# A hybrid decoder block on one core: more stages between the hops of a transposed block, the last gate block transposed on TensorE, and one bias and one mask product per head

## The chip, the cores and the metric

The kernel runs on one core of one Trainium2 chip. The metric is device time in microseconds (us), from launch to end; the median of three runs is 1239.57 us. PE is the matmul engine (TensorE), PEld its weight load, DVE the vector engine, ACT the scalar engine, POOL GpSimd, and SP the engine whose queue issues most of the loads.

## The reference, cut to what matters

One decoder block on a sequence of 256 positions with 2048 channels, all in float32:

```
h    = rms_norm(x) @ w_in                      # attention q, k, v; forget gate; mLSTM q, k, v, i, f, o
attn = softmax(q k^T / sqrt(128) + c_q - c_k, causal) @ v        # 8 heads of 128, c = cumsum(log f)
ht   = mlstm_chunkwise(silu(conv(mq, mk)), mv, i, log f)         # 4 heads, q/k 128, v 256
x   += concat(attn, rms_norm(ht) * sigmoid(mo)) @ w_out
x   += (silu(h2 @ w_gate) * (h2 @ w_up)) @ w_down                # h2 = rms_norm(x), 5632 columns
x   += sigmoid(rms_norm(x) @ w_ple_gate) * rms_norm(p @ w_ple_proj)
```

## The kernel before

Every large product goes through `linear`. The 256 positions are two query blocks of 128, each with a PSUM accumulator of 128 x 512. A weight piece of 256 rows by 512 columns is loaded by SP into `wr` (512 KB), ACT casts it to `wh` (fp32r), and DVE takes the rest, `wl = wr - wh`. Each 128 rows then give three matmuls per query block (L253 to L255: activation high by wh, high by wl, low by wh), so one piece is 12 matmuls. The pool of `wr`, `wh` and `wl` has four buffers of each.

The activations must stand with channels on the partitions, as pairs `act_h` and `act_l` of 512 channels (four of 128) by 256 positions. Two ways lead there:

- `transposed` goes by hops. DVE transposes 32 x 32 squares into `tq` (two instructions), ACT's queue issues four stores to a DRAM tile `swap` (L191) and one load from it into `quad` (L195), and `split` takes high and low parts from `quad` (ACT L133 or L129, DVE L135 or L130). `tq` and `quad` have one buffer each, and the list `held` lets only one block be under way.
- `transpose_in` transposes on TensorE, four 128 x 128 products with the identity (L165) into a PSUM tile `tr`, then `split`; it does two channel groups at a time. The first activations and the second half of the mLSTM output go this way.

Such side work is written as tasks, generators that `advance` steps: before each weight piece `linear` calls `advance(width)`, which takes one step of up to `width` tasks (2 in most linears, 1 in the feed-forward part and w_down). Each `yield` is the end of a step. Before a linear uses an activation block whose task is not done, it steps the tasks until it is. The order of instructions on each engine is fixed when the program is built, from the dependences and the program's order as a priority, so an instruction can be placed ahead of earlier ones; at run time each engine keeps its order.

Stages in order: the projections of w_in (with attention, convolution and mLSTM as tasks beside them), w_out, eleven chunks of gate and up, w_down, four short linears of w_ple_proj (one piece each, results `e` copied by ACT at L678, squared by the task `e_norm`), and w_ple_gate with the output. `residual` runs w_out ("ffn") and w_down ("ple") in four chunks of 512 columns: the DVE addition into `xres` (L616), then the task `after`, whose hops give the activation block for the next product. The block of w_down's chunk 3 is needed by w_ple_gate's seventh piece.

For the heads, `bias_mms` adds to the scores of query block b the bias product of a one-row selector `sel` with the table `R` (128 or 256 columns, L473) and the product of a bf16 identity with the bf16 mask `maskb` (128 columns, L474). `attn` runs the q-k products before it (L541, two instructions each in the trace), `mlstm` keeps bias and q-k products in two tiles (q-k at L495).

Of the kernel before, what the change touches and what calls it, by code (L numbers as in the profile page):

```python
# [14 lines left out]
P = 128  # L15
EPS = 1e-6
NEG = -1e30


def block_kernel(ctx, tc, x, p, w_norm_mix, w_in, fox_f_bias, q_norm_w, k_norm_w, conv_w, conv_b,  # L20
# [147 lines left out]
    def transpose_in(dst, srcs, k0, n, scales=None):  # L168

        for j0 in range(0, n, 2):  # L170
            if j0:
                yield
            t = transpose_pair(lambda b, j: srcs(b, j0 + j))
            split(dst, k0 + j0, 2, t, scales and scales[j0:j0 + 2])

    held = []

    def transposed(srcs):

        while held:
            yield held
        held.append(srcs)
        t = quads.tile([P, 2, 4, 4, 32], F32, name="tq")
        for b in range(2):
            nc.vector.transpose(t[:, b], srcs(b).rearrange("p (k j c) -> p j k c", k=4, j=4))
        yield
        d = dram.tile([4, 32, 2, 4, P], F32, name="swap")
        for i in range(4):  # L190
            nc.scalar.dma_start(out=d[:, :, :, i, :].rearrange("j c b e -> c b j e"),  # L191
                                in_=t[32 * i:32 * i + 32].rearrange("c b j k r -> c b j (k r)"))
        yield
        q = quads.tile([P, 8, 4, 32], F32, name="quad")
        nc.scalar.dma_start(out=q.rearrange("p t k r -> p (t k r)"), in_=d.rearrange("j c b i e -> (j c) (b i e)"))  # L195
        yield
        return q.rearrange("p t k r -> p k t r")

    def split_by_blocks(dst, srcs, scales=None):

        tv = yield from transposed(srcs)
        for k in range(0, 4, 2):
            split(dst, k, 2, tv[:, k:k + 2], scales and scales[k:k + 2])
            if not k:
                yield
        held.pop()
# [52 lines left out]
    with tc.tile_pool(name="mixp", bufs=1) as mp:  # L259
# [125 lines left out]
        for c in range(3):  # L385
            po = linear(w_in, acts_x, 4104 + c * 344, 344)
            for b in range(2):
# [7 lines left out]
        Ch = mp.tile([P, P], F32, name="Ch")  # L395
        sel = mp.tile([P, 12], F32R, name="sel")
        identb = mp.tile([P, P], BF16, name="identb")
        maskb = mp.tile([P, P], BF16, name="maskb")
        nc.gpsimd.memset(ones, 1.0)
        nc.gpsimd.affine_select(out=Ut, in_=ones, compare_op=ALU.is_ge, fill=0.0, base=0, pattern=[[1, P]],  # L400
                                channel_multiplier=-1)
# [2 lines left out]
                                channel_multiplier=-1)  # L404
        nc.gpsimd.tensor_tensor(out=Uc, in0=Ut, in1=Ch, op=ALU.add)
        nc.gpsimd.tensor_tensor(out=Un, in0=Ut, in1=ones, op=ALU.subtract)
        nc.gpsimd.memset(maskb, 0.0)
        nc.gpsimd.affine_select(out=maskb, in_=maskb, compare_op=ALU.is_ge, fill=NEG, base=0, pattern=[[-1, P]],
                                channel_multiplier=1)
        make_identity(nc, identb)  # L410
        sel0 = mp.tile([P, 12], F32, name="sel0")
        nc.gpsimd.memset(sel0, 0.0)
# [54 lines left out]

        NK = (P, 2 * P)

        def bias_mms(t, b, h, start):  # L470

            r0 = 0 if b == 0 else 128
            nc.tensor.matmul(t[:, b, 0:NK[b]], sel[:, h:h + 1].broadcast_to([P, P]), R[:, r0:r0 + NK[b]], start=start, stop=False)  # L473
            nc.tensor.matmul(t[:, b, b * P:(b + 1) * P], identb, maskb, start=False, stop=True)  # L474

        def transpose_probs(src):

# [9 lines left out]
        rh = mp.tile([P, 2, 4], F32, name="rh")  # L487

        def mlstm(h):
            pD = ps.tile([P, 2, 256], F32, name="sc")  # L490
            for b in range(2):
                bias_mms(pD, b, 8 + h, True)
            pS = ps.tile([P, 2, 256], F32, name="sc")
            for b in range(2):
                nc.tensor.matmul(pS[:, b, 0:NK[b]], cv[:, h, b * P:(b + 1) * P], cv[:, 4 + h, 0:NK[b]], start=True, stop=True)  # L495
            mx = small.tile([P, 2], F32, name="mx")
            eb = small.tile([P, 2], F32, name="eb")
            em = small.tile([P, 2], F32, name="em")
            den = small.tile([P, 2], F32, name="den")
            for b in range(2):  # L500
                nc.vector.tensor_reduce(mx[:, b:b + 1], pD[:, b, 0:NK[b]], axis=AX.X, op=ALU.max)
            nc.vector.tensor_tensor(mx, mx, ncT[:, :, h], op=ALU.subtract)
            nc.vector.scalar_tensor_tensor(mx, nBT[:, :, h], -1.0, mx, op0=ALU.mult, op1=ALU.max)
            nc.vector.scalar_tensor_tensor(eb, ncT[:, :, h], -1.0, mx, op0=ALU.mult, op1=ALU.subtract)
            nc.scalar.activation(em, mx, AF.Exp, scale=-1.0)
            W = mp.tile([P, 2, 256], F32, name="prob", bufs=2)
            for b in range(2):
                nc.scalar.activation(W[:, b, 0:NK[b]], pD[:, b, 0:NK[b]], AF.Exp, bias=eb[:, b:b + 1])
                nc.vector.scalar_tensor_tensor(W[:, b, 0:NK[b]], pS[:, b, 0:NK[b]], 1.0, W[:, b, 0:NK[b]],
                                               op0=ALU.mult, op1=ALU.mult, accum_out=den[:, b:b + 1])  # L510
            nc.vector.scalar_tensor_tensor(den, den, -1.0, den, op0=ALU.mult, op1=ALU.max)
            nc.vector.tensor_tensor(den, den, em, op=ALU.max)
            nc.vector.reciprocal(den, den)
            yield
            WT = transpose_probs(W)
            yield
            ph = ps.tile([P, 2, 256], F32, name="tr")
            vs = slice(h * 256, (h + 1) * 256)
            nc.tensor.matmul(ph[:, 0, :], WT[:, 0:128], sB[:, 0, vs], start=True, stop=True)
            nc.tensor.matmul(ph[:, 1, :], WT[:, 128:256], sB[:, 0, vs], start=True, stop=False)  # L520
            nc.tensor.matmul(ph[:, 1, :], WT[:, 256:384], sB[:, 1, vs], start=False, stop=True)
            for b in range(2):
                nc.scalar.activation(hm[:, b, vs], ph[:, b, :], AF.Copy, scale=den[:, b:b + 1])
                sumsq(ssh[:, b, h:h + 1], hm[:, b, vs])
# [11 lines left out]
        acts_m = [None] * 4  # L536

        def attn(h, qT, kT, v):
            t = ps.tile([P, 2, 256], F32, name="sc")
            for b in range(2):  # L540
                nc.tensor.matmul(t[:, b, 0:NK[b]], qT[:, h % 4, b * P:(b + 1) * P], kT[:, h % 4, 0:NK[b]], start=True,  # L541
                                 stop=False)
                bias_mms(t, b, h, False)
            nm = small.tile([P, 2], F32, name="nm")
            rsum = small.tile([P, 2], F32, name="rsum")
            pb = mp.tile([P, 2, 256], F32, name="prob", bufs=2)
            for b in range(2):
                nc.vector.tensor_reduce(nm[:, b:b + 1], t[:, b, 0:NK[b]], axis=AX.X, op=ALU.max, negate=True)
                nc.scalar.activation(pb[:, b, 0:NK[b]], t[:, b, 0:NK[b]], AF.Exp, bias=nm[:, b:b + 1],
                                     accum_out=rsum[:, b:b + 1])  # L550
            nc.vector.reciprocal(rsum, rsum)
            for b in range(2):
                nc.vector.tensor_scalar(pb[:, b, 0:NK[b]], pb[:, b, 0:NK[b]], rsum[:, b:b + 1], None, ALU.mult)
            yield
            pT = transpose_probs(pb)
            yield
            o = ps.tile([P, 1, 256], F32, name="tr")
            vs = slice((h % 4) * P, (h % 4 + 1) * P)
            nc.tensor.matmul(o[:, 0, :], v[:, 0, vs], pT[:, 0:256], start=True, stop=False)  # L559
            nc.tensor.matmul(o[:, 0, 128:256], v[:, 1, vs], pT[:, 256:384], start=False, stop=True)  # L560
            split(acts_m[h // 4], h % 4, 1, o)
# [34 lines left out]
        def residual(w, acts, voff, name, pieces=None):  # L596

            ss = const.tile([P, 2, 4], F32, name="ss_" + name)
            rstd = const.tile([P, 2], F32, name="rstd_" + name)

            def after(c, dst):
                scales = [vec_b[:, voff + c * 4 + j:voff + c * 4 + j + 1] for j in range(4)]
                yield from split_by_blocks(dst, lambda b: xres[:, b, c * 512:(c + 1) * 512], scales)
                for b in range(2):
                    sumsq(ss[:, b, c:c + 1], xres[:, b, c * 512:(c + 1) * 512])
                if c == 3:
                    ssr = small.tile([P, 2], F32, name="ssr")
                    nc.vector.tensor_reduce(ssr, ss, axis=AX.X, op=ALU.add)
                    rsqrt(rstd, ssr, 1.0 / D, [P, 2])

            nxt = []
            for c in range(4):
                cs = slice(c * 512, (c + 1) * 512)
                po = linear(w, acts, c * 512, 512, pieces=pieces, width=1 if pieces else 2)
                for b in range(2):
                    nc.vector.tensor_tensor(xres[:, b, cs], po[b], xres[:, b, cs], op=ALU.add)  # L616
                nxt.append(new_act())
                made_by[id(nxt[c][0])] = Task(after(c, nxt[c]))
            return nxt, rstd
# [104 lines left out]
```

## Time and profile before

| | us |
|---|---|
| median of three runs (lowest, highest) | 1239.57 (1239.51, 1240.84) |
| the profiled execution's own time | 1238.18 |
| its span, first to last instruction | 1236.5 |
| PE busy | 1219.0 |
| DVE busy | 708.2 |
| ACT busy | 587.7 |

The span is what the profiler saw between the first and the last instruction; the device time has 1.7 us around it. Busy time is the union of an engine's instructions. Matmuls overlap in the records and their ends are modelled, so a busy PE is not a PE at its best rate: the distance from one start to the next tells more. In the rows below, the bracket at the end of a timeline row is the idle time of the engine just before it and what ended it; x2 or x4 means that neighbouring instructions of one line were merged.

### The profile page before, as it was taken

To read this page: it belongs to the slowest core of one execution; us is meant where nothing else is said; L and a number is where in the kernel's file an instruction comes from. 1 tells how busy PE (TensorE), PEld (TensorE's weight loads), DVE (VectorE), ACT (ScalarE), POOL (GpSimd) and SP (SyncE) were. 2 spreads that over 40 slices of the span, in tenths; PEclk is the share of its full clock that TensorE was granted. 3 is DMA by queue.
4 is the path that set the end of the run, shared out by engine and by line. 5 is a ranking of instruction groups with operands and counts; after the bars stand their busy time and mean duration, and the time that the engine had idled before them with its cause. 6 is when DMAs were issued, how large, how long until landed. Compare 5 with 4: busy or idle time off the path is not lost.

```text
span 1236.5 us, 15306 instructions
## 1 busy us (share of the span) xinstructions
PE 1219.0 (99%) x5691; PEld 1020.2 (83%) x5691; DVE 708.2 (57%) x950; ACT 587.7 (48%) x822; POOL 4.1 (0%) x23
## 2 busy tenths in 40 slices
PE   9999999999999999999999999999999999998998
PEld 6799977888888888888888888888888888887788
DVE  5567655565665755555555555556545554544764
ACT  6655555555545534444443443444344444445542
POOL 1000000000000000000000000000000000000000
PEclk9999999999999999999999999999999999999999
DMA  7577754665678776777777777677766666765772
GB/s 259 175 239 230 223 158 120 187 214 165 216 230 255 226 223 201 232 209 215 227 222 213 213 223 219 201 227 221 221 211 211 210 212 203 224 198 172 221 242 90
DMA packets 160013, 258.35 MB, mean 209 GB/s; under 512 B 10082, under 2 KB 56004, under 8 KB 159940
## 3 DMA queue, kind: packets, MB, share of 16 engines
q1 hardware_dynamic: 127156, 229.06, 60.4%
q10 hardware_dynamic: 32784, 28.33, 7.5%
q8 instruction: 44, 0.72, 0.2%
q14 instruction: 29, 0.24, 0.1%
HBM read 241.62 MB, written 15.73 MB: 208 GB/s over the span
## 4 chain that ended last, share of the span: by engine, by line
PE 80%; ACT 2%; DMA 2%; DVE 1%; issue 0%; ACTq 0%; DVEq 0%
PE acc L254 26%; PE acc L255 26%; PE acc L253 26%; DMA swap<-tq 1%; DMA quad<-swap 1%; ACT sq L116 1%; DVE wl L229 0%; ACT wh L228 0%; PE sc L541 0%; DMA wr<-in_w_in_dram 0%; PE tr L559 0%; ACT qs L344 0%; ACTq L191 0%; PE tr L479 0%; PE sc L495 0%
## 5 line engine op out<-in xcount | busy, mean ns | idle before, releaser
L229 DVE TENSOR_TENSOR wl<-wr,wh 128x1024 fp32r<-128x1024 f32 (+2 forms) x445 | 521.3, 1181 | 409.4 <-ACT wh L228 408.6
L228 ACT CAST wh<-wr 128x1024 fp32r<-128x1024 f32 (+2 forms) x445 | 448.0, 1018 | 518.8 <-PE acc L255 370.9
L253 PE MATMUL acc<-wh,act_h 128*128 128x512 f32 (+2 forms) x1568 | 592.9, 379 | 5.7 <-ACT wh L228 4.6
L254 PE MATMUL acc<-wl,act_h 128*128 128x512 f32 (+2 forms) x1568 | 592.2, 378 | 4.7 <-DVE wl L229 4.7
L255 PE MATMUL acc<-wh,act_l 128*128 128x512 f32 (+2 forms) x1568 | 591.9, 377 | 0.0
L254 PEld LDWEIGHTS acc<-wl,act_h 128*128 128x128 f32 x1568 | 295.3, 188 | 57.5 <-DVE wl L229 6.9
L253 PEld LDWEIGHTS acc<-wh,act_h 128*128 128x128 f32 x1568 | 294.7, 188 | 57.9 <-ACT wh L228 5.7
L255 PEld LDWEIGHTS acc<-wh,act_l 128*128 128x128 f32 x1568 | 295.0, 188 | 51.8 <-DVE act_l L135 0.6
L253 PE MATMUL acc<-wh,gh 128*128 128x512 f32 x224 | 88.0, 393 | 0.0
L254 PE MATMUL acc<-wl,gh 128*128 128x512 f32 x224 | 87.9, 393 | 0.0
L255 PE MATMUL acc<-wh,gl 128*128 128x512 f32 x224 | 87.1, 389 | 0.0
L255 PEld LDWEIGHTS acc<-wh,gl 128*128 128x128 f32 x224 | 42.0, 188 | 9.5
L253 PEld LDWEIGHTS acc<-wh,gh 128*128 128x128 f32 x224 | 42.1, 188 | 9.4
L254 PEld LDWEIGHTS acc<-wl,gh 128*128 128x128 f32 x224 | 42.1, 188 | 8.6
L133 ACT ACTIVATE act_h<-quad,vec_b 128x256 fp32r<-128x256 f32 x36 | 15.5, 499 | 23.1 <-DMA quad<-swap 23.1
L135 DVE SCALAR_TENSOR_TENSOR act_l<-quad,vec_b,act_h 128x256 fp32r<-128x256 f32 x36 | 15.3, 483 | 17.6 <-ACT act_h L133 17.6
L637 ACT ACTIVATE gg<-acc,rstd_ffn 128x512 f32<-128x512 f32 x22 | 15.1, 689 | 10.8 <-PE acc L255 10.8
L638 DVE SCALAR_TENSOR_TENSOR gg<-acc,rstd_ffn,gg 128x512 f32<-128x512 f32 x22 | 15.8, 751 | 4.9 <-ACT gg L637 4.9
L130 DVE TENSOR_TENSOR gl<-quad,gh 128x512 fp32r<-128x512 f32 x14 | 9.1, 688 | 16.3 <-ACT gh L129 16.3
L129 ACT CAST gh<-quad 128x512 fp32r<-128x512 f32 x14 | 8.0, 618 | 20.5 <-DMA quad<-swap 20.5
L641 DVE SCALAR_TENSOR_TENSOR gg<-acc,rstd_ffn,gg 128x512 f32<-128x512 f32 x22 | 15.4, 744 | 0.0
L116 ACT ACTIVATE sq<-xres 128x512 bf16<-128x512 f32 x24 | 14.9, 622 | 0.0
(192 smaller groups left out, 398.1 us busy)
## 6 DMA issues: line engine op xcount, KB each, us to landing
wr<-in_w_ffn_gate_dram SPq DMA_DIRECT2D x88, 512.0 KB, 3.8
wr<-in_w_ffn_up_dram SPq DMA_DIRECT2D x88, 512.0 KB, 4.6
wr<-in_w_ffn_down_dram SPq DMA_DIRECT2D x88, 512.0 KB, 4.6
wr<-in_w_in_dram SPq DMA_DIRECT2D x63, 512.0 KB, 4.5
wr<-in_w_in_dram SPq DMA_DIRECT2D x48, 344.0 KB, 3.7
wr<-in_w_out_dram SPq DMA_DIRECT2D x32, 512.0 KB, 4.7
wr<-in_w_ple_gate_dram SPq DMA_DIRECT2D x32, 512.0 KB, 5.0
swap<-tq ACTq DMA_DIRECT2D x104, 128.0 KB, 4.2
```

The source lines that it names most:

```text
L116: nc.scalar.activation(sq[:, 0:n], src, AF.Square, accum_out=dst)
L130: nc.vector.tensor_tensor(lo, src, hi.bitcast(F32), op=ALU.subtract)
L133: nc.scalar.activation(part(dst[0], k + j, 1), src[:, j:j + 1], AF.Copy, scale=scales[j])
L135: nc.vector.scalar_tensor_tensor(part(dst[1], k + j, 1), src[:, j:j + 1], scales[j], part(dst[0], k + j, 1).bitcast(F32), op0=ALU.mult, op ...
L228: nc.scalar.copy(wh, wr)
L229: nc.vector.tensor_tensor(wl, wr, wh.bitcast(F32), op=ALU.subtract)
L253: nc.tensor.matmul(po[b][:, 0:n], ah[:, kk, s], wh[:, j, :], start=count == 1, stop=False)
L254: nc.tensor.matmul(po[b][:, 0:n], ah[:, kk, s], wl[:, j, :], start=False, stop=False)
L255: nc.tensor.matmul(po[b][:, 0:n], al[:, kk, s], wh[:, j, :], start=False, stop=count == total)
L637: nc.scalar.activation(gg[b], pg[b], AF.Sigmoid, scale=r)
L638: nc.vector.scalar_tensor_tensor(gg[b], pg[b], r, gg[b], op0=ALU.mult, op1=ALU.mult)
L641: nc.vector.scalar_tensor_tensor(gg[b], pu[b], rstd2[:, b:b + 1], gg[b], op0=ALU.mult, op1=ALU.mult)
```

## The change

Three edits go together.

- `transposed` takes a parameter `gap` (2 unless given). After the swap issues and after the quad issue it now ends `gap` steps in place of one. `split_by_blocks` hands it on; chunk 3 of w_out keeps gap 1.
- Chunk 3 of w_down, the last block, goes through `transpose_in`: eight TensorE transposes from `xres`, with no hop through DRAM.
- Scores stand in one tile of 512 columns: block 0 in columns 0 to 127, block 1 in 128 to 383 (`keys`). One bias product of 384 columns and one mask product of 256 (columns 0 to 127 and 256 to 383, from a mask of two copies, made by one more instruction on POOL) serve both query blocks. In `attn` the bias comes first, then the q-k products, then the mask.

```diff
-    def transposed(srcs):
+    def transposed(srcs, gap=2):
...
             nc.scalar.dma_start(out=d[:, :, :, i, :].rearrange("j c b e -> c b j e"),
                                 in_=t[32 * i:32 * i + 32].rearrange("c b j k r -> c b j (k r)"))
-        yield
+        for _ in range(gap):
+            yield
         q = quads.tile([P, 8, 4, 32], F32, name="quad")
         nc.scalar.dma_start(out=q.rearrange("p t k r -> p (t k r)"), in_=d.rearrange("j c b i e -> (j c) (b i e)"))
-        yield
+        for _ in range(gap):
+            yield
         return q.rearrange("p t k r -> p k t r")
...
-        tv = yield from transposed(srcs)
+        tv = yield from transposed(srcs, gap)
...
-        def bias_mms(t, b, h, start):
-
-            r0 = 0 if b == 0 else 128
-            nc.tensor.matmul(t[:, b, 0:NK[b]], sel[:, h:h + 1].broadcast_to([P, P]), R[:, r0:r0 + NK[b]], start=start, stop=False)
-            nc.tensor.matmul(t[:, b, b * P:(b + 1) * P], identb, maskb, start=False, stop=True)
+        def keys(t, b):
+
+            return t[:, 0:P] if b == 0 else t[:, P:3 * P]
+
+        def bias_mm(t, h):
+
+            nc.tensor.matmul(t[:, 0:3 * P], sel[:, h:h + 1].broadcast_to([P, P]), R, start=True, stop=False)
+
+        def mask_mm(t):
+
+            nc.tensor.matmul(t.rearrange("p (a c) -> p a c", c=P)[:, 0:3:2, :], identb, maskb2, start=False, stop=True)
...
-            pD = ps.tile([P, 2, 256], F32, name="sc")
-            for b in range(2):
-                bias_mms(pD, b, 8 + h, True)
+            pD = ps.tile([P, 512], F32, name="sc")
+            bias_mm(pD, 8 + h)
+            mask_mm(pD)
...
-            t = ps.tile([P, 2, 256], F32, name="sc")
-            for b in range(2):
-                nc.tensor.matmul(t[:, b, 0:NK[b]], qT[:, h % 4, b * P:(b + 1) * P], kT[:, h % 4, 0:NK[b]], start=True,
-                                 stop=False)
-                bias_mms(t, b, h, False)
+            t = ps.tile([P, 512], F32, name="sc")
+            bias_mm(t, h)
+            for b in range(2):
+                nc.tensor.matmul(keys(t, b), qT[:, h % 4, b * P:(b + 1) * P], kT[:, h % 4, 0:NK[b]], start=False, stop=False)
+            mask_mm(t)
...
-                yield from split_by_blocks(dst, lambda b: xres[:, b, c * 512:(c + 1) * 512], scales)
+                if c == 3 and name == "ple":
+                    yield from transpose_in(dst, lambda b, j: xres[:, b, c * 512 + j * P:c * 512 + (j + 1) * P], 0, 4, scales)
+                else:
+                    yield from split_by_blocks(dst, lambda b: xres[:, b, c * 512:(c + 1) * 512], scales, 1 if c == 3 else 2)
```

## Rows read from the trace of the kernel before

**Rows 1.** The page, busy time by engine (us, share, instructions).

```profile
PE 1219.0 (99%) x5691; PEld 1020.2 (83%) x5691; DVE 708.2 (57%) x950; ACT 587.7 (48%) x822; POOL 4.1 (0%) x23
```

**Rows 2.** PE's timeline, last gate block (start, us, instruction, idle before).

```profile
1136.84 0.39 PE L255 MATMUL acc<-wh,pl 128*128 128x512 f32 x1
1138.18 0.73 PE L253 MATMUL acc<-wh,act_h 128*128 128x512 f32 x2 [0.95 <-ACT wh L228]
...
1139.77 0.39 PE L255 MATMUL acc<-wh,act_l 128*128 128x512 f32 x1
...
1141.61 0.39 PE L255 MATMUL acc<-wh,act_l 128*128 128x512 f32 x1
1143.70 0.73 PE L253 MATMUL acc<-wh,act_h 128*128 128x512 f32 x2 [1.70 <-ACT wh L228]
...
1145.56 0.63 PE L255 MATMUL acc<-wh,act_l 128*128 128x512 f32 x1
...
1148.12 0.46 PE L253 MATMUL acc<-wh,act_h 128*128 128x512 f32 x1
```

**Rows 3.** PE's waits: who for whom, us in total, times, longest.

```profile
PE acc L254 <- DVE wl L229: 4.7, 6, 2.0
PE acc L253 <- ACT wh L228: 4.6, 3, 1.9
```

**Rows 4.** The waits of all engines, ACT's for the stores to swap.

```profile
ACT wh L228 <- DMA swap<-tq: 44.2, 19, 3.0
```

**Rows 5.** Window of 20 us (busy us by engine, granted clock, DMA share, GB/s).

```profile
1140.00:1160.00 20.00, 17.77 (x70) 13.93 (x69) 13.78 (x26) 13.18 (x25) 0.00 (x0) 0.91 0.68 203
```

**Rows 6.** ACT's timeline, last gate block (ACTq is its sequencer).

```profile
1129.03 1.93 ACTq L191 DMA_DIRECT2D swap<-tq  x3
...
1135.48 0.33 ACTq L195 DMA_DIRECT2D quad<-swap  x1
1135.86 0.63 ACT L116 ACTIVATE sq<-act_h 128x512 bf16<-128x512 f32 x1 [0.75 <-DMA swap<-tq]
...
1137.10 1.03 ACT L228 CAST wh<-wr 128x1024 fp32r<-128x1024 f32 x1
1138.82 0.91 ACT L133 ACTIVATE act_h<-quad,vec_b 128x256 fp32r<-128x256 f32 x2 [0.70 <-DMA quad<-swap]
...
1142.61 1.04 ACT L228 CAST wh<-wr 128x1024 fp32r<-128x1024 f32 x1
```

**Rows 7.** Chain of waits, the mLSTM output's second block on TensorE.

```profile
320.88 0.44 PE tr L165 x4
```

**Rows 8.** PE's timeline, one mLSTM head and one attention head.

```profile
169.43 0.22 PE L473 MATMUL sc<-R,sel 128*128 128x128 f32 x1
...
169.80 0.87 PE L495 MATMUL sc<-m 128*128 128x128 f32 x4
170.33 0.58 PE L253 MATMUL acc<-wh,act_h 128*128 128x512 f32 x1
...
281.04 0.30 PE L473 MATMUL sc<-R,sel 128*128 128x128 f32 x1
...
282.13 0.30 PE L473 MATMUL sc<-R,sel 128*128 128x128 f32 x1
```

**Rows 9.** PE's timeline, 256-column matmuls of the last linear.

```profile
1224.83 0.28 PE L255 MATMUL acc<-wh,act_l 128*128 128x256 f32 x1
...
1227.95 0.28 PE L254 MATMUL acc<-wl,act_h 128*128 128x256 f32 x1
```

**Rows 10.** PE's timeline, its two long stalls beside the projections.

```profile
59.48 0.59 PE L253 MATMUL acc<-wh,act_h 128*128 128x344 f32 x2 [1.90 <-ACT wh L228]
...
114.92 0.43 PE L254 MATMUL acc<-wl,act_h 128*128 128x344 f32 x1 [2.00 <-DVE wl L229]
```

**Rows 11.** DVE's timeline after the convolution steps.

```profile
113.99 3.23 DVE L229 TENSOR_TENSOR wl<-wr,wh 128x688 fp32r<-128x688 f32 x4
```

**Rows 12.** PE's timeline, first scores of the second half.

```profile
269.60 0.49 PE L541 MATMUL sc<-qkT 128*128 128x128 f32 x2 [0.33 <-ACT qkT L326]
```

More of the change, by code (lines that the diff above doesn't have):

```diff
@@ L192, in transposed, with split_by_blocks @@
                                 in_=t[32 * i:32 * i + 32].rearrange("c b j k r -> c b j (k r)"))
-        yield
+        for _ in range(gap):
+            yield
         q = quads.tile([P, 8, 4, 32], F32, name="quad")
         nc.scalar.dma_start(out=q.rearrange("p t k r -> p (t k r)"), in_=d.rearrange("j c b i e -> (j c) (b i e)"))
-        yield
+        for _ in range(gap):
+            yield
         return q.rearrange("p t k r -> p k t r")
-    def split_by_blocks(dst, srcs, scales=None):
-        tv = yield from transposed(srcs)
+    def split_by_blocks(dst, srcs, scales=None, gap=2):
+        tv = yield from transposed(srcs, gap)
         for k in range(0, 4, 2):
@@ L397, in block_kernel @@
         identb = mp.tile([P, P], BF16, name="identb")
-        maskb = mp.tile([P, P], BF16, name="maskb")
+        maskb2 = mp.tile([P, 2, P], BF16, name="maskb")
         nc.gpsimd.memset(ones, 1.0)
@@ L406, in block_kernel @@
         nc.gpsimd.tensor_tensor(out=Un, in0=Ut, in1=ones, op=ALU.subtract)
-        nc.gpsimd.memset(maskb, 0.0)
-        nc.gpsimd.affine_select(out=maskb, in_=maskb, compare_op=ALU.is_ge, fill=NEG, base=0, pattern=[[-1, P]],
-                                channel_multiplier=1)
+        nc.gpsimd.memset(maskb2, 0.0)
+        for b in range(2):
+            nc.gpsimd.affine_select(out=maskb2[:, b, :], in_=maskb2[:, b, :], compare_op=ALU.is_ge, fill=NEG, base=0,
+                                    pattern=[[-1, P]], channel_multiplier=1)
         make_identity(nc, identb)
@@ L489, in mlstm @@
         def mlstm(h):
-            pD = ps.tile([P, 2, 256], F32, name="sc")
+            pD = ps.tile([P, 512], F32, name="sc")
+            bias_mm(pD, 8 + h)
+            mask_mm(pD)
+            pS = ps.tile([P, 512], F32, name="sc")
             for b in range(2):
-                bias_mms(pD, b, 8 + h, True)
-            pS = ps.tile([P, 2, 256], F32, name="sc")
-            for b in range(2):
-                nc.tensor.matmul(pS[:, b, 0:NK[b]], cv[:, h, b * P:(b + 1) * P], cv[:, 4 + h, 0:NK[b]], start=True, stop=True)
+                nc.tensor.matmul(keys(pS, b), cv[:, h, b * P:(b + 1) * P], cv[:, 4 + h, 0:NK[b]], start=True, stop=True)
             mx = small.tile([P, 2], F32, name="mx")
@@ L500, in mlstm @@
             for b in range(2):
-                nc.vector.tensor_reduce(mx[:, b:b + 1], pD[:, b, 0:NK[b]], axis=AX.X, op=ALU.max)
+                nc.vector.tensor_reduce(mx[:, b:b + 1], keys(pD, b), axis=AX.X, op=ALU.max)
             nc.vector.tensor_tensor(mx, mx, ncT[:, :, h], op=ALU.subtract)
@@ L507, in mlstm @@
             for b in range(2):
-                nc.scalar.activation(W[:, b, 0:NK[b]], pD[:, b, 0:NK[b]], AF.Exp, bias=eb[:, b:b + 1])
-                nc.vector.scalar_tensor_tensor(W[:, b, 0:NK[b]], pS[:, b, 0:NK[b]], 1.0, W[:, b, 0:NK[b]],
+                nc.scalar.activation(W[:, b, 0:NK[b]], keys(pD, b), AF.Exp, bias=eb[:, b:b + 1])
+                nc.vector.scalar_tensor_tensor(W[:, b, 0:NK[b]], keys(pS, b), 1.0, W[:, b, 0:NK[b]],
                                                op0=ALU.mult, op1=ALU.mult, accum_out=den[:, b:b + 1])
@@ L547, in attn @@
             for b in range(2):
-                nc.vector.tensor_reduce(nm[:, b:b + 1], t[:, b, 0:NK[b]], axis=AX.X, op=ALU.max, negate=True)
-                nc.scalar.activation(pb[:, b, 0:NK[b]], t[:, b, 0:NK[b]], AF.Exp, bias=nm[:, b:b + 1],
+                nc.vector.tensor_reduce(nm[:, b:b + 1], keys(t, b), axis=AX.X, op=ALU.max, negate=True)
+                nc.scalar.activation(pb[:, b, 0:NK[b]], keys(t, b), AF.Exp, bias=nm[:, b:b + 1],
                                      accum_out=rsum[:, b:b + 1])
```

## The prediction

> **What bounds the kernel.** I read the page first, then PE's waits, then PE's timeline wherever two neighbouring matmuls start further apart than their length explains. PE is busy for 1219.0 of 1236.5 us [rows 1]. Busy times are modelled, so the spacing of the starts has to be seen too: in the undisturbed stretch from 1139.77 to 1141.61 us nine 512-column matmuls start within 1.84 us, eight intervals of 0.23 us [rows 2]. That spacing holds through the feed-forward part. What PE loses to other engines is small and sits in a few places: its two largest waits come to 4.7 us (for wl) and 4.6 us (for wh) in the whole run [rows 3]. So only two kinds of edit can move the time: fewer or shorter PE instructions, and the removal of a stall that really reaches PE. ACT's waits for swap come to 44.2 us over 19 places [rows 4], but wpool holds four pieces and a piece is 12 matmuls, 12 x 0.23 = 2.76 us of PE, so a 3.0 us wait alone never empties PE's stock. The reader should not take those 44 us for a gain.
>
> **The last gate block.** It belongs to chunk 3 of w_down ("ple"), and its hops run while PE does the four short w_ple_proj pieces and starts w_ple_gate. From 1136.84 to 1148.12 us PE starts 22 matmuls in 11.28 us; at 0.23 us they are worth 5.06 us, so 6.2 us are lost [rows 2]. They split as follows:
> - 1136.84 to 1138.18, waiting for the first gate piece's wh: 1.34 - 0.23 = 1.1 us; the two matmuls that follow and the wait for wl, to 1139.77: 1.59 - 0.69 = 0.9 us.
> - 1141.61 to 1143.70, the second piece's wh: 2.09 - 0.23 = 1.9 us; from 1143.70 to 1145.56 another 1.86 - 0.69 = 1.2 us.
> - 1145.56 to 1148.12: six intervals of 0.43 us, 6 x 0.20 = 1.2 us. After these stalls the granted clock fell to the lower of its two levels (1.2 of 2.4 GHz); the 20 us window has 0.91 [rows 5].
>
> ACT is what is late. Three of four swap issues hold its sequencer for 1.93 us from 1129.03, the quad issue at 1135.48 waits for the swap, squares follow 0.75 us after ACT fell idle, and only then the first gate cast (1137.10); before the second cast (1142.61) stand four scaled copies from quad, which waited for its landing too [rows 6].
>
> Removed: two DVE transposes, four swap issues, one quad issue, both landings. Added: eight TensorE transposes. Their price is the row of the mLSTM output's block, which already goes this way: 0.44 us for four [rows 7], so 0.9 us. The copies into act_h and act_l stay, four each, now from PSUM, and no longer stand behind a landing. Suppose ACT's order stays otherwise as it is. The first cast comes 0.75 us earlier, so 0.75 of 2.0 us of the first stall goes. The four quad copies (two pairs of 0.91 us, the first after a 0.70 us wait: 2.5 us [rows 6]) leave the way of the second cast, which had made PE wait 1.70 us [rows 2]. That takes all of 1.9 + 1.2, and with it the slow stretch of 1.2 us, which only followed the stalls. That is 5.0 us back. If casts also move ahead, all 6.2 are. Less 0.9 us: a gain of 4.1 to 5.3; I take 4.3, since the kept order is the nearer reading. The lower bound is 0: the transposes wait for both xres additions, and they could stand in PE's queue ahead of the w_ple_proj matmuls. In the mLSTM block they were put between big matmuls and PE did not stop [rows 7], which speaks against it.
>
> **One bias and one mask product.** Per head four instructions become two, at the same 640 columns (128 + 128 + 256 + 128 before, 384 + 256 after). One attention head repeats every 282.13 - 281.04 = 1.09 us; the same q-k products alone take 170.33 - 169.80 = 0.53 us in the mLSTM head, so bias and mask take 0.56 us there, and 169.80 - 169.43 = 0.37 us in an mLSTM head [rows 8]. The floor is the columns alone: 27 matmuls of 256 columns start from 1224.83 to 1227.95, 0.12 us each [rows 9], so 640 columns are 0.30 us. The gain is between nothing and 8 x 0.26 + 4 x 0.07 = 2.4 us. The excess belongs to switches between the mask's bf16 identity and the other weights; half the switches stay, so I take half, 1.2 us.
>
> The Trainium skill, page "TensorE: Matmul & The Clock Gate", section "Back-to-back issue gap", gives a warm gap of N/2.4 + 2.5 ns. As an estimate from it, the four products are 0.277 us and the two 0.272 us, which over 12 heads saves 0.06 us and would make the whole sum 4.96 us instead of 6.1. It speaks against this part of the change; the trace does not agree with it here (0.56 and 0.37 us measured), and no run shows the merged form yet.
>
> One price the merge has: both blocks' maxima now wait for one mask product at the end. It is about 0.5 us more for the first block's chain, beside big matmuls that fill PE; uncovered it is at most 12 x 0.5 = 6 us, which I do not expect. The second mask on POOL is made in the first microseconds and used after 169 us: nothing.
>
> **More stages.** One stage is one weight piece (2.76 us of PE). In 24 of the 26 transposed blocks (ffn chunk 3 keeps its gap, the last block leaves) the swap stays where it is, quad goes one stage later and the copies two. No instruction is added. ACT stands less long at quad. PE could see that only where it stalls: 1.9 us before 59.48 and 2.0 us before 114.92 [rows 10]. The first waits for a cast that stands behind the squares of k, which the change leaves there. The second waits for wl, which DVE only reaches at 113.99 us, after a batch of convolution steps [rows 11]; these start with the quad block and move by two stages, so the stall goes or moves along. I count a third of it, 0.6 us; the bounds are 2.0 us lost (a second such batch) and 3.9 us gained (both stalls).
>
> What comes later must still be in time. An up-chunk has seven steps now in place of five, and eight pieces in the next linear; in the w_down order the newest block is wanted after 12 pieces. In the w_out stage the block of chunk 3 keeps five steps for six pieces. So no linear has to wait for a block by program order.
>
> **Sum.** 4.3 + 1.2 + 0.6 = 6.1 us. The profiled execution took 1238.18 us, its span 1236.5 and 1.7 around it: 1232.1. It is 1.4 us under the median of the runs shown, so the median after is 1233.5 us.
>
> **Rivals.**
> - *Half of the stall stays.* The casts come free of the landing but stay behind the four pairs of squares, 1.2 us each; then 2 us come back instead of 4.3. With 1.2 and nothing from the stages: 1239.57 - 3.2 = 1236.4. For it: the squares stand directly ahead of both casts now [rows 6]. Against: they fit between pieces once the quad copies have gone.
> - *The change does not do what it says.* The order on an engine is not the program's (the first gate cast, 1137.10, stands before the first scaled copies, 1138.82, which the program has earlier [rows 6]), so stalls may just come at another place: transposes 0.9 us, stall moved elsewhere, merge 1.2: 1239.3, and anything within 2.5 us of no change.
> - *Slower.* The second half's attention already meets late data: at 269.60 PE waited 0.33 us for the k block's copy from quad [rows 12]. q and k go through the hops one after the other and come up to two stages later each. If the score products keep their place in PE's fixed order, PE stands for 4 x 2.76 = 11 us: 1239.57 - 6.1 + 11 = 1244.5. It decides from 6.1 + 2.5 = 8.6 us of waiting. Against: the head's work is written after the copy in the program and moves with it, and its result is wanted only in w_out, tens of us later.
>
> **How the numbers follow.** Forecast 0.60, half of the stall 0.17, no effect 0.16, slower 0.07. About 0.2% (2.5 us) is what a measurement of this kernel tells from no change. Faster by over that, under 1237.1: the first two and little of the third, 0.77; the same: 0.16; slower: 0.07. The range leaves out the slower rival and some of each end: 1230.5 (5.3 + 2.4 + 1.4) to 1238.5. The forecast's own range is 1231 to 1236.
>
> **What would show it.** Right: no wait of PE of over 0.5 us between 1125 and 1150 us and a granted clock of 1.00 there, eight more transposes on TensorE at 0.11 us, 24 fewer small matmuls, under 0.9 us a head, 100 swap and 25 quad issues; the feed-forward part as long as before. Wrong: casts of the gate weights still behind squares; PE waiting for the transposes before w_ple_proj; a wait at the scores of the second half; a stall at the convolutions as long as before or twice.

## The result

The changed kernel takes 1228.57 us (median of four runs, 1228.42 to 1229.32). In the same session the kernel before took 1240.2 us (1239.51 to 1241.11). The ratio is 0.9907 [0.989, 0.9924]: faster by 0.9%. All ratios in this document are of fast executions; a single slow one, 4358 us in the experiment with only the squares put later, is left out. The forecast was 1233.5 us with 1230.5 to 1238.5 as range, so the direction was right and the size was not: the gain is 4.9 us larger than forecast, and the time lies under the range.

The 4.9 us have two halves. The profiled execution after takes 1229.32 us where the sum gave 1232.1, which is 2.8 us. And the median of the runs, which stood 1.4 us above the profiled execution before, stands 0.75 us below it after, which is 2.15 us. The second half is not in any term of the sum, and the experiments had to explain it too.

The page after, busy time by engine, answers to [rows 1]:

```profile
PE 1215.7 (99%) x5675; PEld 1017.9 (83%) x5675; DVE 706.0 (58%) x948; ACT 585.9 (48%) x822; POOL 4.5 (0%) x24
```

PE has 16 instructions fewer: 24 small products fewer, eight transposes more, as forecast. The span fell from 1236.5 to 1227.6 us, 8.9 us, though PE's busy time fell by 3.3 only; the rest was idle time. PE's waits after (who for whom; us in total, times, longest) answer to [rows 3]:

```profile
PE acc L255 <- ACT wh L230: 1.9, 1, 1.9
PE acc L256 <- DVE wl L231: 1.5, 3, 0.6
```

The waits for wh went from 4.6 to 1.9 us, those for wl from 4.7 to 1.5. To see where, I set the starts of the same instructions of both traces side by side:

| stretch | before, us | after, us | gain |
|---|---|---|---|
| convolution: ACT's sixth copy into sA to its second into sB | 17.44 | 15.51 | 1.9 |
| second copy into sB to the second sigmoid for `sg` (attention and mLSTM heads) | 174.16 | 172.15 | 2.0 |
| w_out, feed-forward part, w_down | 829.7 | 829.7 | 0.0 |
| last gate block: w_down's last addition to the second sigmoid of w_ple_gate | 39.05 | 33.63 | 5.4 |
| from there to the end | 71.0 | 71.6 | -0.6 |

**The last gate block.** PE's timeline after, with the eight transposes and the end of the w_ple_proj matmuls, answers to [rows 2]:

```profile
1122.48 0.31 PE L165 MATMUL tr<-ident,xres 128*128 128x128 f32 x1
...
1123.10 0.50 PE L165 MATMUL tr<-ident,xres 128*128 128x128 f32 x3
...
1125.29 0.60 PE L165 MATMUL tr<-ident,xres 128*128 128x128 f32 x4
...
1133.75 0.40 PE L257 MATMUL acc<-wh,pl 128*128 128x512 f32 x1
1133.99 0.39 PE L255 MATMUL acc<-wh,act_h 128*128 128x512 f32 x1
```

The first gate matmul (L255, from `act_h`) follows 0.24 us after the last one of w_ple_proj: PE does not stop. Around the transposes PE's 14 intervals from 1122.01 to 1126.20 us take 4.19 us where 14 x 0.23 = 3.2 are due, so eight transposes cost 1.0 us. ACT's timeline shows the reason. Before, beside [rows 6], the copies of the first three results `e`:

```profile
1128.47 1.14 ACT L678 COPY act_h<-acc 128x512 f32<-128x512 f32 x2
...
1131.08 1.27 ACT L678 COPY act_h<-acc 128x512 f32<-128x512 f32 x2 [1.47 <-PE acc L255]
1133.83 1.27 ACT L678 COPY act_h<-acc 128x512 f32<-128x512 f32 x2 [1.47 <-PE acc L255]
```

and after:

```profile
1125.12 1.07 ACT L690 COPY act_h<-acc 128x512 f32<-128x512 f32 x2
1126.06 0.86 ACT L133 ACTIVATE act_h<-tr,vec_b 128x256 fp32r<-128x256 f32 x2
...
1128.48 1.08 ACT L230 CAST wh<-wr 128x1024 fp32r<-128x1024 f32 x1
...
1131.15 1.10 ACT L690 COPY act_h<-acc 128x512 f32<-128x512 f32 x2
1132.09 1.10 ACT L230 CAST wh<-wr 128x1024 fp32r<-128x1024 f32 x1
```

The scaled copies into `act_h` are done before 1127 us, and the gate's first two casts stand at 1128.48 and 1132.09 us, behind two and four of the eight squares of e. Before, they stood behind two and four squares as well. What changed is where the copies of e stand, which wait for PE's products: before, three of the four pairs and the quad issue were ahead of the first cast (1137.10), after only one pair and a half. The granted clock is 1.00, the higher of its two levels (2.4 GHz), where [rows 5] had 0.91 (window of 20 us: busy us by engine, clock, DMA share, GB/s):

```profile
1140.00:1160.00 20.00, 20.00 (x90) 16.57 (x89) 14.43 (x23) 8.27 (x9) 0.00 (x0) 1.00 0.68 225
```

**The heads.** PE's timeline after, one attention head, beside [rows 8]:

```profile
202.59 0.42 PE L479 MATMUL sc<-R,sel 128*128 128x384 f32 x1
202.86 0.82 PE L551 MATMUL sc<-qkT 128*128 128x128 f32 x4
203.51 0.27 PE L483 MATMUL sc<-maskb,identb 128*128 128x256 bf16 x1
203.54 0.48 PE L255 MATMUL acc<-wh,act_h 128*128 128x512 f32 x1
```

A head now takes 203.54 - 202.59 = 0.95 us in place of 1.09. Before, these products stood between the two rows of [rows 8] at 281.04 and 282.13 us:

```profile
281.19 0.23 PE L474 MATMUL sc<-maskb,identb 128*128 128x128 bf16 x1
281.26 0.65 PE L541 MATMUL sc<-qkT 128*128 128x256 f32 x2
281.56 0.47 PE L473 MATMUL sc<-R,sel 128*128 128x256 f32 x1
281.87 0.23 PE L474 MATMUL sc<-maskb,identb 128*128 128x128 bf16 x1
281.94 0.44 PE L541 MATMUL sc<-qkT 128*128 128x128 f32 x2
```

From one start to the next, the two bias products took 0.15 + 0.31 = 0.46 us, the two masks 0.07 each and the q-k products 0.30 + 0.19 = 0.49. Now they take 0.27, 0.03 and 0.65. The saving sits in the merged products; the q-k products got 0.16 us longer, and the traces do not say why. The large product behind the last mask followed 0.04 us after it before as well (282.95 and 282.99 us). Over the eight attention heads the mean is 0.91 us, with 0.86 where a head stands right behind a large product.

**The convolution.** The stall before 114.92 us [rows 10] has no successor. DVE's timeline shows why. Before (the batch that ends at the row of [rows 11]):

```profile
107.94 0.74 DVE L370 TENSOR_SCALAR m<-m,vec_b 128x256 f32<-128x256 f32 x2 [0.70 <-ACT m L364]
108.60 2.46 DVE L374 SCALAR_TENSOR_TENSOR m<-m,vec_b,m 128x256 f32<-128x256 f32 x6
110.97 0.73 DVE L370 TENSOR_SCALAR m<-m,vec_b 128x256 f32<-128x256 f32 x2
111.62 2.46 DVE L374 SCALAR_TENSOR_TENSOR m<-m,vec_b,m 128x256 f32<-128x256 f32 x6
```

and after:

```profile
108.14 0.74 DVE L372 TENSOR_SCALAR m<-m,vec_b 128x256 f32<-128x256 f32 x2 [1.03 <-ACT m L366]
108.80 0.87 DVE L231 TENSOR_TENSOR wl<-wr,wh 128x688 fp32r<-128x688 f32 x1
109.58 1.67 DVE L376 SCALAR_TENSOR_TENSOR m<-m,vec_b,m 128x256 f32<-128x256 f32 x4
111.16 0.87 DVE L231 TENSOR_TENSOR wl<-wr,wh 128x688 fp32r<-128x688 f32 x1
```

Before, 16 convolution steps run for 6 us in one batch and the wl come after it. After, two wl stand between the steps, in DVE's built order. The steps start at the same time (107.94 and 108.14 us): they were not run later, the order around them changed. ACT's order changed too, and a wl needs its wh first. Before, the second block's four swap issues came in one go, ahead of the next casts:

```profile
106.79 2.94 ACTq L191 DMA_DIRECT2D swap<-tq  x4
109.83 2.10 ACT L228 CAST wh<-wr 128x688 fp32r<-128x688 f32 x3 [2.00 <-DVE m L374]
```

After, two casts stand ahead of the last three issues:

```profile
107.94 1.61 ACT L230 CAST wh<-wr 128x688 fp32r<-128x688 f32 x2
108.79 1.91 ACTq L191 DMA_DIRECT2D swap<-tq  x3
```

No run separates the two changes of order.

### The profile page after: what moved, and what is told of

Read it like the earlier page. It is cut to its first block, busy times and chain, and to the rows that moved or that the text cites. A ratio compares the mean times of both kernels' runs of the same rounds, so it can differ in the third digit from the quotient of the medians.

```text
span 1227.6 us, 15262 instructions
## 1 busy us (share of the span) xinstructions
PE 1215.7 (99%) x5675; PEld 1017.9 (83%) x5675; DVE 706.0 (58%) x948; ACT 585.9 (48%) x822; POOL 4.5 (0%) x24
## 4 chain that ended last, share of the span: by engine, by line
PE 88%; DMA 4%; DVE 3%; ACT 2%; issue 1%; ACTq 0%; SPq 0%; DVEq 0%
PE acc L256 29%; PE acc L257 28%; PE acc L255 28%; DMA wr<-in_w_in_dram 3%; DVE wl L231 1%; DMA wpost<-in_w_ple_post_norm_dram 1%; ACT wh L230 1%; ACT sq L116 1%; DMA quad<-swap 0%; DMA swap<-tq 0%; DVE m L376 0%; PE sc L551 0%; ACT act_h L690 0%; PE tr L165 0%; PE tr L568 0%
## 5 line engine op out<-in xcount | busy, mean ns | idle before, releaser
L255 PE MATMUL acc<-wh,act_h 128*128 128x512 f32 (+2 forms) x1568 | 593.1, 379 | 3.2 <-ACT wh L230 1.9
L255 PEld LDWEIGHTS acc<-wh,act_h 128*128 128x128 f32 x1568 | 294.6, 188 | 55.3 <-ACT wh L230 2.2
L255 PE MATMUL acc<-wh,gh 128*128 128x512 f32 x224 | 88.0, 393 | 0.0
L255 PEld LDWEIGHTS acc<-wh,gh 128*128 128x128 f32 x224 | 42.1, 188 | 9.4
```

The lines of the kernel that those rows point to most:

```text
L255: nc.tensor.matmul(po[b][:, 0:n], ah[:, kk, s], wh[:, j, :], start=count == 1, stop=False)
```

## The experiments

All ratios are to the kernel before on the same chip; the chip differs between some of the experiments.

**Each edit alone.** Three kernels with one edit each tell which term of the sum was too small. First, before with the last block on TensorE only:

```diff
-                yield from split_by_blocks(dst, lambda b: xres[:, b, c * 512:(c + 1) * 512], scales)
+                if c == 3 and name == "ple":
+                    yield from transpose_in(dst, lambda b, j: xres[:, b, c * 512 + j * P:c * 512 + (j + 1) * P], 0, 4, scales)
+                else:
+                    yield from split_by_blocks(dst, lambda b: xres[:, b, c * 512:(c + 1) * 512], scales)
```

> Before, with the last gate block alone transposed on TensorE. Account by stages (each edit brings what its own stage shows in the two profiles): span 5.0 us shorter than before's 1236.5, all of it after 1125 us, the convolution stall at 113 us as long as before; and if the 2.7 us by which the runs moved more than the profiles also belong to this stage, 7 to 8 us in the runs. Rival (the three edits only reshuffle the order together): under 3 us.

Measured: 0.9968 [0.9955, 0.998], so 4.0 us [2.5, 5.6]. Its last-block stretch is 33.63 us, the same as after: 5.4 us less than before. The gain is under the 5 us that were expected and far from 7 to 8. In its profile, whose span is only 3.2 us under the first of the kernel before, the clock fell after the stalls near 59 and 115 us.

Second, before with the stages only (gap 2, and 1 for chunk 3 of w_out and w_down):

```diff
-    def transposed(srcs):
+    def transposed(srcs, gap=2):
...
-        yield
+        for _ in range(gap):
+            yield
```

> Before, with the additional stages alone (last block and w_out's chunk 3 keep theirs). Account by stages: 2.0 us from the stall at the convolutions and about 0.5 us at the first scores of the second half, so 2 to 2.5 us, the last gate block's stall of 6.2 us unchanged. Rival (reshuffling): within 1 us of before, or the stall at another place.

Measured: 0.9970 [0.996, 0.998], 3.7 us [2.5, 5.0]. The convolution stretch is 15.57 us as after, and the first scores of the second half wait for nothing. The gain is above the 2 to 2.5 us expected.

Third, the merge only (after with gap 1 and the last block by hops):

```diff
-    def transposed(srcs, gap=2):
+    def transposed(srcs, gap=1):
...
-    def split_by_blocks(dst, srcs, scales=None, gap=2):
+    def split_by_blocks(dst, srcs, scales=None, gap=1):
...
-                if c == 3 and name == "ple":
-                    yield from transpose_in(dst, lambda b, j: xres[:, b, c * 512 + j * P:c * 512 + (j + 1) * P], 0, 4, scales)
-                else:
-                    yield from split_by_blocks(dst, lambda b: xres[:, b, c * 512:(c + 1) * 512], scales, 1 if c == 3 else 2)
+                yield from split_by_blocks(dst, lambda b: xres[:, b, c * 512:(c + 1) * 512], scales)
```

> Before, with the one bias and one mask product per head alone. Account by stages: an attention head 0.95 us on TensorE in place of 1.09, so 1.1 us for eight, up to 0.4 us for the four mLSTM heads, 1.2 to 1.5 us in all, and the convolution stall unchanged. By the page's gap rule for TensorE 0.06 us. Rival (reshuffling): the convolution stall goes here too, 3 us or more.

Measured: 0.9979 [0.9966, 0.9992], 2.6 us [1.0, 4.2]. The stretch of the heads is 1.6 us shorter; the convolution's stall (2.34 us) and the last block's loss are there. The three gains multiply to 0.9917, within the interval of the whole change: the edits hardly touch each other.

**The kernel before once more**, with a profile of its own, because single profiles of these kernels did not add up:

> The kernel before, unchanged, once more. Its profiled execution was 1.4 to 3 us under its other runs, while the changed kernel's was 0.7 us above. If the last gate block's stall differs between executions (with the lower clock held longer), spans spread by 1 to 3 us here and a second profile shows that stretch longer than 11.3 us for 22 matmuls; if it is the profiling, the second profile looks like the first and the runs stay 1 to 3 us above it.

Measured: 1.0008 [0.9999, 1.0017]; its span is 1237.6 us, 1.1 more than the first profile, with stalls at the same places. They are not of the same length: the convolution stretch takes 17.81 us in place of 17.44 (PE waits 2.32 us, not 2.00), and the last gate block 39.87 in place of 39.05 (ACT waits 1.98 us for the swap, not 0.75). The clock differs too. The windows of 60 to 80 us, first execution and then second:

```profile
60.00:80.00 20.00, 18.76 (x118) 18.42 (x118) 12.71 (x24) 9.64 (x14) 0.00 (x0) 1.00 0.84 255
```

```profile
60.00:80.00 20.00, 19.93 (x117) 19.93 (x118) 12.09 (x24) 8.84 (x13) 0.00 (x0) 0.91 0.80 241
```

The stall before 60 us is in both, but only in the second did the granted clock fall after it. In this place it shows little: the second execution had been 0.6 us ahead, the first has a further wait of 0.64 us in the window (hence its lower busy time), and by 64 us both are level. So a stall has a price of its own and, in some executions, a second one; its size is read from another window below.

**Where the stages act.** Gap 2 in the two convolution blocks alone, and everywhere but there:

```diff
         def conv(j0):
-            tv = yield from transposed(lambda b: sA[:, b, 8 + j0 * P:8 + (j0 + 4) * P])
+            tv = yield from transposed(lambda b: sA[:, b, 8 + j0 * P:8 + (j0 + 4) * P], 2)
```

> Before, with the additional stages in the two convolution blocks alone. If the stages pay by taking the batch of convolution steps apart from the casts: the PE stall of 2.0 to 2.5 us near 113 us goes, 2 us in the span, and 2.5 to 3.5 us in the runs since the clock no longer falls after it in some of them; everything after 150 us as before. Rival (every block brings a little, by shorter waits of ACT): under 1 us.

> Before, with the additional stages in all blocks but the two of the convolution (last block and w_out's chunk 3 as before). By the convolution reading: the stall near 113 us stays, at most 0.5 to 1 us from the first scores of the second half and the k block, runs within 1 us of before. By the rival: 2.5 us or more, ACT's waits for swap well under 44 us and the gain spread over the run.

Measured: 0.9980 [0.9968, 0.9993] and 0.9991 [0.998, 1.0002]. With the first the convolution stretch is 15.58 us and no wait over 0.2 us is left there; with the second the stall stays (1.79 us). Together (-0.20% and -0.09%) they give what the second experiment gave (-0.30%), two thirds of it from the convolution; the second alone does not stand clear of no change. Both lie near what the convolution reading expected. In the first one's profile the scores of the second half waited far longer than before [rows 12] (PE's timeline):

```profile
270.84 0.49 PE L543 MATMUL sc<-qkT 128*128 128x128 f32 x2 [3.02 <-ACT qkT L328]
```

and the clock fell after it (0.91 from 260 to 280 us), so this execution, at 1238.8 us, is one of the two longest of its kernel's twelve. The q/k blocks alone with gap 2:

```diff
-            tv = yield from transposed(lambda b: s[:, b, :])
+            tv = yield from transposed(lambda b: s[:, b, :], 2)
```

> Before, with the additional stages in the four q and k blocks alone. If the second part of what the stages bring is PE's wait at the second half's first scores (0.3 to 3.2 us in the profiles so far with the old stages, none with the new): no wait over 0.2 us there, 1 to 2 us off the runs, the convolution stall as long as before. Rival: the wait stays and the time is as before.

Measured: 0.9992 [0.9982, 1.0002]: no wait of the scores in its profile, the convolution's stall as before (2.29 us), and a gain too small for the interval.

**Why the last block lost time.** Two kernels keep its hops through DRAM. One gives them two stages each; the other issues them on SP's queue in place of ACT's:

```diff
+                yield from split_by_blocks(dst, lambda b: xres[:, b, c * 512:(c + 1) * 512], scales,
+                                           2 if c == 3 and name == "ple" else 1)
```

> Before, with the additional stages in the last gate block alone, still by hops. If it is the wait for the landings in ACT's order that delays the gate casts, more stages cure it too: PE's loss of 6.2 us around 1140 us falls under 2 us and the kernel is 3 to 5 us faster. If it is the hold of ACT by the four swap issues, the loss stays at 4 us or more and the kernel gains at most 1.5 us.

```diff
-            nc.scalar.dma_start(out=d[:, :, :, i, :].rearrange("j c b e -> c b j e"),
+            queue.dma_start(out=d[:, :, :, i, :].rearrange("j c b e -> c b j e"),
...
+                                           nc.sync if c == 3 and name == "ple" else None)
```

> Before, with the last gate block's five hop issues on SP's queue in place of ACT's. If the five issues in ACT's order are what keeps the gate casts back: PE's loss around 1140 us falls from 6.2 us to under 3 us and the kernel is 2 to 4 us faster, unless the gate loads, now behind the issues on SP, come late in their place. If it is the copies of the projection results and the squares: the loss stays at 5 us or more, the time as before.

Measured: 1.0002 [0.9992, 1.0013] for the stages and 0.9944 [0.9932, 0.9956] for the queue, 6.9 us, where 2 to 4 were expected. ACT's timeline with two stages:

```profile
1130.80 1.91 ACTq L191 DMA_DIRECT2D swap<-tq  x3
...
1138.07 0.33 ACTq L196 DMA_DIRECT2D quad<-swap  x1
1138.44 1.18 ACT L681 COPY act_h<-acc 128x512 f32<-128x512 f32 x2 [1.57 <-PE acc L257]
...
1140.75 1.03 ACT L230 CAST wh<-wr 128x1024 fp32r<-128x1024 f32 x1
```

The first gate cast is at 1140.75 us, later still, behind all four pairs of copies of e and two squares; PE waits 2.84 us for it. ACT's timeline with the hops on SP's queue:

```profile
1132.99 1.03 ACT L229 CAST wh<-wr 128x1024 fp32r<-128x1024 f32 x1
...
1136.59 1.07 ACT L229 CAST wh<-wr 128x1024 fp32r<-128x1024 f32 x1
...
1143.19 0.90 ACT L133 ACTIVATE act_h<-quad,vec_b 128x256 fp32r<-128x256 f32 x2
```

The same hops, the same squares, but the first cast stands behind one pair of copies of e only, 10 us ahead of the copies from quad, and PE has no wait between 1125 and 1150 us. The stretch takes 32.63 us, 6.4 less than before and 1.0 less than with TensorE: just the transposes' price. The casts come early with the issues off ACT's queue, and late with them on it. Whether that is the time that ACT spends on the issues, or only the order that is built around them, is not separated.

**The stall before 59 us**, which the change leaves (1.90 us of idle PE in both traces). The prediction put it down to the squares of k ahead of the cast. Two more yields before those squares, in the changed kernel and in the kernel before:

```diff
-        def qk_norm(s, dT, vec):
+        def qk_norm(s, dT, vec, late=0):
+            for _ in range(late):
+                yield
...
+            return dT, Task(qk_norm(s, dT, qs_w if which == "q" else vec_b[:, v_k:v_k + 1], 2 if c0 == 1024 else 0),
+                            [tasks["params"]])
```

> The changed kernel, with the first k block's squares put two stages later, so that the cast of the next projection's second piece stands ahead of them. If PE's remaining stall near 57 us (2.1 and 0.8 us) is that order on ACT: it falls to about 1 us, 2 us off the span of 1227.6 and a granted clock of 1.00 between 50 and 80 us; ratio to before about 0.989. Rival: the casts wait for weights or buffers there, no change against the changed kernel.

> Before, with the first k block's squares two stages later and nothing else. If the stall near 57 us is their place on ACT: it falls from 2.8 us to about 0.5 us, 2 to 2.5 us off the span, no lower clock between 55 and 70 us, and so 3 to 4 us in the runs. Rival (it pays only together with the stages): under 1 us.

Measured: 0.9870 [0.9853, 0.9887], median 1224.39 us, for the changed kernel, and 0.9986 [0.9975, 0.9997] for the kernel before. PE's waits of the first:

```profile
PE sc L49 <- DVE tq L44: 1.3, 1, 1.3
PE acc L255 <- ACT act_h L133: 0.8, 1, 0.8
PE acc L256 <- DVE wl L231: 0.8, 3, 0.4
```

No wait for wh is left. The spans of its four executions lie within 0.3 us (1222.5 to 1222.8) at a clock of 1.00, where those of the kernel before lie between 1235.5 and 1245.7 us in 88 runs. In the kernel before the same yields bring 2.3 us by 105 us, and 1.5 of them are gone after the convolution, whose stall is still there and after which the clock fell in this profile. The runs of this kernel gained 1.7 us [0.4, 3.1], under the 3 to 4 expected.

**The best of both**: the changed kernel with those yields and with the last block by hops on SP's queue.

> The changed kernel with the squares of the first k block later and the last gate block by hops again, its issues on SP's queue. If what kept the gate casts back was only the place of the issues in ACT's order, the eight TensorE transposes (0.9 us) are no longer needed: span 1221.6 us or 0.9 us under the 1222.5 of the version with the squares alone, runs 0.986 of before, the clock at 1.00. If the gate loads now come late behind the hops on SP, PE waits near 1130 to 1145 us and it is slower than that version by 1 us or more.

Measured: 0.9849 [0.9824, 0.9873], median 1223.30 us. It is the fastest, though not apart from 0.9870 by the intervals. In its profile a convolution stall is back (PE's timeline):

```profile
114.56 0.42 PE L257 MATMUL acc<-wl,act_h 128*128 128x344 f32 x1 [1.66 <-DVE wl L232]
```

so what the stages do there hangs on the order that is built for each kernel, not on the stages as such.

## Why the prediction was too small

**Where stalls sit, and what they are worth.** The 14 profiles give the convolution stretch (as in the table above) in three kinds, and the last gate block's likewise:

| stretch | no long stall | stall, clock 1.00 | stall, then a lower clock |
|---|---|---|---|
| convolution | 15.51 to 15.62 (4 profiles) | 17.05 to 17.87 (5) | 18.70 to 19.28 (5) |
| last gate block | 33.63 on TensorE (3), 32.63 on SP (2) | 37.19 to 37.71 (2) | 38.48 to 40.16 (7) |

A stall of 2 us at the convolution costs 1.4 to 2.4 us, and 3.1 to 3.8 where the clock fell. For the lower clock alone, the window of 100 to 120 us tells. The second profile of the kernel before, and then the kernel with the last block on TensorE only, which is the same code up to there:

```profile
100.00:120.00 20.00, 17.68 (x113) 17.39 (x112) 15.76 (x28) 11.13 (x15) 0.00 (x0) 1.00 0.78 240
```

```profile
100.00:120.00 20.00, 17.68 (x103) 17.40 (x102) 15.74 (x28) 11.11 (x15) 0.00 (x0) 0.91 0.78 240
```

The same stall (2.32 us in both) and the same busy time, but 10 matmuls of 0.16 us fewer in the second, 1.6 us. The first profiled execution of before had one stretch at the lower clock (at 1140 us); nine of the other profiles had two or three, and four had none (the changed kernel, its two successors, and the stages alone). In 88 runs of the kernel before the median span is 1236.05 us at a mean granted clock of 0.999 (4 runs), 1237.45 at 0.997 (20) and 1240.8 at 0.994 (9).

Point by point:

- *What bounds the kernel* was right. ACT's 44 us of waits for swap cost PE nothing in the feed-forward part, and every gain is a PE stall or a shorter PE sequence.
- *Last gate block, 4.3 us:* 5.4 in the profile, 4.0 [2.5, 5.6] by the runs of that edit alone. The mechanism was right, the casts behind hops and copies on ACT. The choice "the kept order is the nearer reading" was wrong: the casts kept their two and four squares, but moved ahead of copies of e that wait for PE. All 6.2 us came back, and the transposes took 1.0 of them (0.9 forecast). That the place of the hops' issues on ACT held the casts back is shown by the two kernels with hops: on another queue all is back, with more stages nothing. Why the order is built so was not looked into.
- *One bias and one mask product, 1.2 us:* 2.6 [1.0, 4.2] by the runs, 1.6 to 2.0 in the profiles. "Half the switches stay, so I take half" was mis-sized, and that the excess belongs to switches to the bf16 identity is not shown: a large product followed the mask after 0.04 us before and 0.03 after, and what got shorter are the bias products (0.46 to 0.27 us) and the masks (0.14 to 0.03). The floor by columns (2.4 us) was the nearer bound. By the estimate from the Trainium skill, page "TensorE: Matmul & The Clock Gate", section "Back-to-back issue gap", 0.06 us would be saved; the trace does not agree, with 0.14 us saved in a single attention head. That section of the Trainium skill gives its formula for an isolated product and says that it counts too little for short ones. The longer wait of the first block's maxima did not show.
- *More stages, 0.6 us:* this is the term that failed most: 3.7 us [2.5, 5.0]. "The stall goes or moves along. I count a third of it" treated the two outcomes as a draw between known sizes. The step behind it was wrong: the convolution steps did not move by two stages, they start at the same time, and the built order put casts and wl between them. So the stall went altogether (1.9 us in the profile). That it went was in part luck: with the same stages it is back in the last kernel (1.66 us). The prediction also left out that a removed stall takes with it the lower clock that follows in some executions, and that the second half's scores wait longer than the 0.33 us of [rows 12] in others: 3.02, 2.61 and 1.14 us in three of the eight profiles with gap 1 in the q/k blocks, none in the six with gap 2 there.
- *The sum against one profiled execution:* "1.4 us under the median" was carried over as a constant. By the clocks and spans above it is the price of what that execution happened not to have, and it went with the stalls: after, the median is 0.75 us below the profile. Only profiled executions show their stalls, so for the others this is argued.
- *The stall before 59 us* stayed (1.90 us), for the reason given; moving the squares took it away.

The rivals: half of the stall did not stay, although the casts did stay behind squares as that rival said; the squares themselves came 9 us earlier (the first at 1126.78 us, 1135.86 before). That the change does nothing fell with all three parts. The slower rival named the right place and the wrong sign: the copies came later in the program, yet the scores moved with them. They start 4.4 us after the copy of the k block ends (264.87 and 269.29 us), where it was 0.05 us before (269.55 and 269.60).

Of what would show it, most came true: 100 swap and 25 quad issues, 0.12 us a transpose, clock 1.00, no wait over 0.5 us from 1125 to 1150 us, the feed-forward part of the same length. Attention heads take 0.86 to 0.95 us, not all under 0.9. One sign of being wrong, gate casts still behind squares, was there and did no harm.

The 0.6 us given back after the last gate block are two things: at 1164.38 us PE's weight load waits 0.49 us for a wl, which costs 0.34 us, and 0.24 us come after PE's last matmul started, as in the other two kernels with that block on TensorE (5.0 us to the end there, 4.8 in all others). The reason for either is open. So is how often the clock falls after a given stall: it was only counted, over few executions.

## What to carry to other kernels

Where PE is 99% busy, price each stall at its length plus the lower clock that may follow it, and read more than one profile: the first scores' wait was 0.33 and 0.27 us in the two of the kernel before, and 2.61 and 3.02 us in two kernels whose q/k blocks are the same. DMA issues on a computing engine's queue are part of that engine's order: before a hop is rebuilt on another engine, try it on a queue that has nothing to compute. Here that made the stretch 1.0 us shorter than the rebuilt hop did; the runs gave 6.9 us [5.5, 8.4] against 4.0 [2.5, 5.6], on different chips, and these intervals touch. A built order answers to small shifts in the program, so look at where the casts land after every edit.

## What was not expected of the hardware

- The granted clock fell after the convolution's stall in 5 of 10 profiles with that stall, and not in the others, though the stalls were alike (1.66 to 2.34 us). Where it fell, 10 matmuls in 20 us were missing, 1.6 us.
- The same load into quad took 5.1 us in one execution and 7.4 in another, with the same code up to there, from the end of its issue to the copy that waited for it: issued at 262.94, copied at 268.40 us in the kernel before; issued at 262.50, copied at 270.19 us with gap 2 in the last block only. That makes the scores' wait 0.33 us in the one and 2.61 us in the other. Why the load took longer was not looked into. ACT's timeline of the second:

```profile
262.50 0.33 ACTq L196 DMA_DIRECT2D quad<-swap  x1
...
270.19 1.15 ACT L328 ACTIVATE qkT<-quad,vec_b 128x1024 f32<-128x1024 f32 x1 [4.05 <-DMA quad<-swap]
```
